# One decoder layer: a product moved forward, a residual sum cut in two, tail steps moved, a single-block unit put third

## The chip, the cores and the metric

The kernel runs on one core of a Trainium2 chip. The metric is the device time of that core in microseconds (us), from the start of the program to its end; less is better. The median of three runs before the change is 1732.85 us (1726.88, 1732.85 and 1733.94). Each kernel is also profiled once, in an execution of its own; the times of single instructions below all come from that one execution.

The engines are named as the profile names them: PE multiplies matrices (PEld is its loading of weights), DVE and ACT work elementwise, POOL does the same for a few operations, SP starts the transfers (DMA). Each engine takes its own instructions strictly in the order in which the program has them, and waits on semaphores for what the others make.

## The reference, cut to what matters

One layer of a hybrid decoder, for 1024 prompt tokens and 8 x 8 sample tokens (1088 in all), in float32:

```python
h = rmsnorm(x, g_mix_pre) * (1 + scale_m) + shift_m
proj = h @ w_in
sc_b, sc_c, sc_x, z, xbc, dt_raw = jnp.split(proj, idx, axis=-1)
y_sc = sc_b * causal_dwconv(sc_c * sc_x, sc_buf, sc_conv_w)      # short convolution
...                                                              # xbc, dt -> SSD scan -> y_ssd
y_ssd = rmsnorm(grouped(y_ssd * silu(z)), 1.0) * ssm_norm_g
mix = jnp.concatenate([y_sc, y_ssd], axis=-1) @ w_out
x = x + gate_m * rmsnorm(mix, g_mix_post)
h2 = rmsnorm(x, g_ffn_pre) * (1 + scale_f) + shift_f
f = (jax.nn.silu(h2 @ w_gate) * (h2 @ w_up)) @ w_down
x = x + gate_f * rmsnorm(f, g_ffn_post)
```

D_MODEL is 1024, the short-convolution group has 1024 channels, the SSD group 16 heads of 64 in four groups, and the hidden width of the FFN is 2816 (11 blocks of 256).

## The kernel before, in words

**Number format.** A float32 product is made of three matmuls on parts: a value v is split into `hi` (v rounded by a cast on ACT) and `lo` (v - hi, a subtraction on DVE), and hi·hi + hi·lo + lo·hi is summed in PSUM. So every weight tile costs one cast on ACT and one subtraction on DVE before PE can use it (`part`, L1039 and L1040; for whole weight columns `split_w`, L311 and L312). The third matmul of a group of three is the one that needs the `lo` part of the weight (L1080 in a product, L336 in a plain sum `acc3`).

**Units of seven products.** Most of the large matrix products are done as *units*: a 256-column strip of a weight against all tokens, cut 2 x 2, with seven half-size products instead of eight (the products are numbered 1 to 7 as in Strassen's scheme). `combos_w` (L1042) loads the strip as two `raw` tiles and makes the seven weight combinations with additions on DVE (one of them on POOL where `eng` says so) and a `part` for each; it takes the tiles from a ring (`in_turn(w_from)`). `unit` (L1082) walks the table `ORDER`, the sequence of products 1, 5, 6, 3, 7, 2, 4; for each entry and each of the two token blocks q it issues one `product` (24 or 12 matmuls, `pm` and `pz` being the PSUM tiles of block 0 and 1), and then the evacuation: a copy on ACT (L1093) or an addition on DVE (L1095). `between` names generators of other work of which one step is issued behind product n.

**Short convolution.** For each of four pairs of channel tiles three units run (`sc_unit`: the columns of sc_c at 1024, of sc_x at 2048, of sc_b at 0). Between their products stand the steps of `norm`, the grouped norm of the SSD output (groups 2 and 3 are still open when the first unit starts): squares on ACT and DVE (L929, L930), sums of squares by six-matmul groups on PE (L920), then the reciprocal root, twelve small DVE instructions (`rsqrt_of`, L279 to L285, on a tile called `sm`), and then `spread`, six-matmul groups on PE that read its result (L291). PE stands still at L291 until the last L285 is done.

**Output projection and tail.** `out_proj` runs 8 plain products for each of three token ranges (L1318 to L1321: three-part sums on PE, an addition on DVE into `acc`), and between them the steps of `mix_tail`, the tail of the mixer: transposes back to token rows (L1239), squares (L1240), a multiplication (L1241), the reciprocal root, the residual sum `x += r * u` on DVE (L1256, four tiles of 128x1024 in the first tail), the sum of squares of the new rows (L357 on ACT), their root, the scaling on ACT (L1348), transposes (L1356), and the evacuation with the FFN norm's factors on ACT (L1358). A dictionary like `{0: [tail], 2: [tail], 5: [tail]}` says behind which product the next step of a generator is issued.

**FFN.** While the tail of the last tokens runs, the first two strips of gate and up are done as plain products (`plain_step`, weights `wp`). One hidden strip of token block 1 is left over (strip 1, `(1, [1])`), then come full units (both blocks) for strips 2 to 9 and two single-block units for strip 10. Each ends in `inner_out`, which writes splits of f to DRAM (`f_d`, L1541) through SP's queue. SP also starts all loads of weight strips (`raw`, L1035) in program order, so a load stands behind every write issued before it. The full units give one of the weight sums to POOL, the single-block ones do all on DVE.

**What sets the order.** The order on PE is that of the code (`chained` and `in_order` tie each step to the PE instruction before it). On ACT and DVE the scheduler of the framework interleaves what depends on nothing earlier, by its own estimate of when an instruction is due; moving a product on PE so also moves weight preparations of ACT and DVE against other work there.

Of the kernel before, what the change touches and what calls it, by code (L numbers as in the profile page):

```python
# [16 lines left out]
P = 128  # L17
# [10 lines left out]
QS = [(0, 256), (512, 288)]  # L28
# [5 lines left out]
def hymba_step(ctx, tc, i, o):  # L34
    nc = tc.nc
# [1003 lines left out]
        nc.scalar.copy(hi, v)  # L1039
        (eng or nc.vector).tensor_tensor(lo, v, hi, op=sub)  # L1040

    def combos_w(w, cols, eng=nc.gpsimd):  # L1042
        raws = [raw_half(w, j, cols) for j in range(2)]
        a11, a12, a21, a22 = (raws[j][:, :, m * P:(m + 1) * P] for m in range(2) for j in range(2))
        W = {}

        def parts_(p, b):
            pl = in_turn(w_from)
            t = pl.tile([P, 2, 4, P], F32R, tag="wc", name=nm(f"w{p}_"))
            part(t[:, 0], t[:, 1], b)  # L1050
            W[p] = [[t[:, s, k] for k in range(4)] for s in range(2)]

        parts_(1, a11)
        parts_(4, a22)
        nc.vector.tensor_tensor(a22, a21, a22, op=add)
        parts_(5, a22)
        eng.tensor_tensor(a21, a11, a21, op=sub)
        nc.vector.tensor_tensor(a11, a22, a11, op=sub)
        parts_(6, a11)
        parts_(2, a12)  # L1060
        nc.vector.tensor_tensor(a12, a12, a11, op=sub)
        parts_(3, a12)
        parts_(7, a21)
        return W
# [14 lines left out]
            mm(ps, W[0][k], X[1][k], start=False, stop=False, skip_group_check=True)  # L1079
            mm(ps, W[1][k], X[0][k], start=False, stop=(stop and k == nk - 1), skip_group_check=True)  # L1080

    def unit(W, X, nk, qs, out, first=True, between={}, blocks_=QS, queue=in_order):  # L1082


        B = {}
        for n, (p, b, new, i, h, opens) in enumerate(ORDER):
            for q in qs:
                if new:
                    B[b, q] = (pm, pz)[q]()
                ps = B[b, q][:, :blocks_[q][1]]  # L1090
                queue(product, ps, W[p], X[q][p], nk, new, p in (3, 2, 4))
                if first and opens:
                    nc.scalar.copy(out(q, i, h), ps)  # L1093
                else:
                    nc.vector.tensor_tensor(out(q, i, h), out(q, i, h), ps, op=add)  # L1095
            for gen in between.get(n, ()):
                if queue is in_order:
                    in_order(next, gen, None)
                else:
                    next(gen, None)  # L1100
# [89 lines left out]
    sums_last()  # L1190


    def sc_unit(cols, tiles, between):
        unit(combos_w(w_in, cols, nc.vector), X_sc, 4, [0, 1],
             lambda q, i, h: tiles[i][:, SQ[q][0] + 272 * h:SQ[q][0] + 272 * (h + 1)], True, between, SQ, chained)

    kept = []
    for pr in range(4):
        cc, cx = [yt((pap, yp2)[pr % 2]) for _ in range(2)], [yt(yp4) for _ in range(2)]
        sc_unit(1024 + 256 * pr, cc, {n: [norms] for n in range(3, 7)})  # L1200
        sc_unit(2048 + 256 * pr, cx, {n: [norms] for n in range(7)})
        if pr == 2:
            conv_state(ncs, 16, 3, o["ssmc_p"], o["ssmc_s"])
        ext = []
        for m in range(2):
            ct = 2 * pr + m
            e = yt(yp4, (P, YT))
            es = e[:, 2 + NP:2 + NP + 80].rearrange("p (b t) -> p b t", b=8)
            nc.vector.tensor_tensor(e[:, 2:2 + NP], cc[m][:, :NP], cx[m][:, :NP], op=mult)
            nc.vector.tensor_tensor(es[:, :, 2:10], bt(cc[m][:, NP:]), bt(cx[m][:, NP:]), op=mult)  # L1210
            keep_tail(e, es, hscT[:, ct, :], nsc[:, ct, :], 2)
            conv(cc[m], e, es, [scw[:, j, ct:ct + 1] for j in range(3)], ct, None)
            ext.append(e)
        cb = [yt(yp4) for _ in range(2)]
        sc_unit(256 * pr, cb, {n: [norms, norms] for n in range(7)})
        for m in range(2):
            y, hi, lo = cc[m], ext[m][:, :T].bitcast(F32R), cb[m].bitcast(F32R)
            nc.vector.tensor_tensor(y, y, cb[m], op=mult)
            split(hi, lo, y)
            kept.append((2 * pr + m, hi, lo))  # L1220
        if pr < 3:
            while kept:
                y_out(*kept.pop(0))


    def size(t):
        return P if t < 8 else NS

    def residual_rows(at, ts, G, res, u, banks, done, parts=((0, 4), (4, 4)), pool=(), halves=(slice(0, D),),
                      squares=None):  # L1230
        ss = smp.tile([P, 3, 12], F32, tag="sm", name=nm("ss"))
        nc.gpsimd.memset(ss, 0.0)
        for j, (k0, nk) in enumerate(parts):
            for tt, t in enumerate(ts):
                tn = size(t)
                cols = slice(k0 * P, (k0 + nk) * P)
                ps = banks[j][tt]()[:tn, :nk * P]
                for k in range(nk):
                    nc.tensor.transpose(ps[:, k * P:(k + 1) * P], at(k0 + k, t), ident)  # L1239
                nc.scalar.activation((squares or u[tt])[:tn, cols], ps, AF.Square, accum_out=ss[:tn, j, tt:tt + 1])  # L1240
                nc.vector.tensor_tensor(u[tt][:tn, cols], ps, (G[0] if t < 8 else G[1])[:tn, cols], op=mult)  # L1241
            if j < len(parts) - 1:
                yield
        n = len(ts)
        for j in range(1, len(parts)):
            nc.vector.tensor_tensor(ss[:, 0, :n], ss[:, 0, :n], ss[:, j, :n], op=add)
        r = rsqrt_of(ss[:, 0, :n], D)
        for tt, t in enumerate(ts):
            tn = size(t)
            for cols in halves:  # L1250
                v, w = res[tt][:tn, cols], u[tt][:tn, cols]
                if tt in pool:
                    nc.scalar.activation(w, w, AF.Copy, scale=r[:tn, tt:tt + 1])
                    nc.gpsimd.tensor_tensor(v, v, w, op=add)
                else:
                    nc.vector.scalar_tensor_tensor(v, w, r[:tn, tt:tt + 1], v, op0=mult, op1=add)  # L1256
                done(t, tn, res[tt], cols)
        yield


# [74 lines left out]
    def mix_tail(ts, x_new, row_new, G):  # L1335
# [5 lines left out]
            nc.sync.dma_start(xn_d[t * P:t * P + tn, :], v[:tn, :])  # L1341
            sum_sq(v, tn, ssn, t, u[t - ts[0]])

        yield from residual_rows(lambda m, t: acc_at(m, t * P, size(t)), ts, G, xr, u, [[pz] * 4] * 2, keep)
        r = rsqrt_of(ssn[:, ts[0]:ts[-1] + 1], D)
        for tt, t in enumerate(ts):
            v = xr[tt][:size(t), :]
# [35 lines left out]
    nxt = next_splits()  # L1383
    out_proj(0, terms[0], {0: [nxt], 2: [nxt]}, out_load)
    tail = mix_tail([0, 1, 2, 3], lambda t: load_x(t, fb, "fm"), rows_fm, G_m)
    out_proj(1, terms[1], {0: [tail], 2: [tail], 5: [tail]}, out_load)
    out_proj(2, terms[2], {1: [tail], 2: [tail]}, out_load, (0, 1))


# [186 lines left out]
    out_proj(2, terms[2], {7: [tail_a]}, lambda mp: w_last, (3,))  # L1576
    tail_b = mix_tail([6, 7, 8], x_tl, row_tl, G2)
    st_from.append(pool(tailp, "stx", 1))
    plain_step(0, 0, ({0: [tail_b], 2: [tail_b], 3: [tail_a]}, {0: [tail_a], 1: [tail_a, mark()], 3: [tail_b]}))
    st_from[:] = [st0]  # L1580
    raw_from = [btp] * 4
    w_from = [slots[1]] * 4 + [slots[0]] * 4
# [23 lines left out]
            "(k p) n -> p k n", p=P))  # L1606
        return raw

    for j, qs in [(1, [1])] + [(j, [0, 1]) for j in range(2, 10)] + [(10, [0]), (10, [1])]:
        eng = nc.gpsimd if len(qs) == 2 else nc.vector  # L1610
        gate_unit(j, qs, combos_w(w_gate, 256 * j, eng))
        W = combos_w(w_up, 256 * j, eng)
# [183 lines left out]
```

## Time and profile before

| | |
|---|---|
| runs (us) | 1726.88, 1732.85, 1733.94; median 1732.85 |
| profiled execution | 1732.75 us, of which the span shown by the profile is 1731.0 us |
| mean granted clock of PE | 0.99 of full speed |
| PE busy | 1682.0 us, 97% of the span, 12604 matmuls |
| DVE, ACT, POOL busy | 1147.9 us (66%), 770.9 us (45%), 185.7 us (11%) |
| read and written | 184.63 MB and 69.71 MB, 147 GB/s over the span |

In rows of instructions the columns are: start in us from the span's start, busy us, engine, line, operation, tile written and tiles read, shapes and types, how many such instructions in a row (x4), and in brackets the idle time of the engine just before and what ended it. In rows of waits: engine, tile and line that waited, who released it, then the total us, the number of waits and the longest. In rows of windows: the stretch in us, its length, then for PE, PEld, DVE, ACT and POOL the busy us with the number of instructions, then the mean granted clock of PE, the share of DMA time, and GB/s.

### The profile page before, as it was taken

How to read it: one execution, taken by the hardware profiler on the slowest of the kernel's cores; microseconds unless marked ns; L12 is line 12 of the kernel's file. 1: busy time of each engine (PE TensorE's matmuls, PEld its weight loads, DVE VectorE, ACT ScalarE, POOL GpSimd, SP SyncE). 2: the span in 40 equal slices, each digit the busy share in tenths (PEclk: the TensorE clock that was granted, in tenths of full speed). 3: DMA queues.
4: the chain of work that ended last, by engine and by line, in shares of the span. 5: the costliest groups of instructions: out<-in, count | busy, mean ns of one | idle time of the engine just before them, and what ended most of it. 6: DMA issues, size and time to landing. Idle time of an engine off the chain costs nothing. (4 is left out here: it accounts for less than half of the span.)

```text
span 1731.0 us, 31270 instructions
## 1 busy us (share of the span) xinstructions
PE 1682.0 (97%) x12604; PEld 1600.0 (92%) x12604; DVE 1147.9 (66%) x2194; ACT 770.9 (45%) x1571; POOL 185.7 (11%) x277
## 2 busy tenths in 40 slices
PE   5999999999999999999999999999999999999997
PEld 4898888899999999998989999999999999999987
DVE  5588677777798776661037779666666658588734
ACT  3457454657544433322226676444444446422222
POOL 2110001000001000000000000122222200122112
PEclk9999999999999999999999999999999999999999
DMA  9201344442322522348275643334433438865523
GB/s 321 73 21 30 113 152 151 148 131 77 109 69 77 177 70 74 113 165 301 69 255 183 195 134 140 121 140 142 147 131 140 148 123 312 314 230 198 203 92 134
DMA packets 159624, 256.37 MB, mean 148 GB/s; under 512 B 10578, under 2 KB 123394, under 8 KB 157943
## 3 DMA queue, kind: packets, MB, share of 16 engines
q1 hardware_dynamic: 159190, 253.19, 42.9%
q8 instruction: 99, 1.62, 0.4%
q10 hardware_dynamic: 288, 1.18, 0.2%
q14 instruction: 47, 0.38, 0.1%
HBM read 184.63 MB, written 69.71 MB: 147 GB/s over the span
## 5 line engine op out<-in xcount | busy, mean ns | idle before, releaser
L312 DVE TENSOR_TENSOR wl<-raw,wh 128x512 fp32r<-128x512 f32 (+1 forms) x87 | 61.3, 729 | 100.3 <-ACT wh L311 89.2
L334 PE MATMUL pm<-h,wh 128*128 128x384 f32 (+1 forms) x342 | 115.1, 337 | 0.1
L335 PE MATMUL pm<-h,wh 128*128 128x384 f32 (+1 forms) x342 | 114.9, 336 | 0.0
L336 PE MATMUL pm<-h,wl 128*128 128x384 f32 (+1 forms) x342 | 114.3, 335 | 0.0
L336 PE MATMUL pm<-hb,wl 128*128 128x512 f32 (+2 forms) x320 | 107.3, 337 | 2.1 <-DVE wl L312 2.1
L311 ACT CAST wh<-raw 128x512 fp32r<-128x512 f32 (+1 forms) x89 | 56.4, 665 | 116.2 <-PE pm L335 68.2
L335 PE MATMUL pm<-hb,wh 128*128 128x512 f32 (+2 forms) x320 | 107.4, 337 | 0.0
L334 PE MATMUL pm<-hb,wh 128*128 128x512 f32 (+2 forms) x320 | 105.8, 338 | 1.0 <-ACT wh L311 1.0
L1039 ACT CAST wd<-raw 128x256 fp32r<-128x256 f32 x112 | 42.9, 406 | 96.1 <-PE pz L1080 33.6
L1040 DVE TENSOR_TENSOR fs<-f,fs 128x576 fp32r<-128x576 f32 (+2 forms) x76 | 52.9, 710 | 25.3 <-ACT fs L1039 24.5
L336 PEld LDWEIGHTS pm<-hb,wl 128*128 128x128 f32 x320 | 60.8, 190 | 7.6 <-DVE wl L312 2.4
L334 PEld LDWEIGHTS pm<-h,wh 128*128 128x128 f32 x342 | 65.5, 191 | 1.9 <-issue 0.9
L335 PEld LDWEIGHTS pm<-h,wh 128*128 128x128 f32 x342 | 65.3, 191 | 1.4 <-issue 0.7
L334 PEld LDWEIGHTS pm<-hb,wh 128*128 128x128 f32 x320 | 60.3, 190 | 6.8 <-ACT wh L311 1.2
L336 PEld LDWEIGHTS pm<-h,wl 128*128 128x128 f32 x342 | 65.2, 191 | 1.3 <-issue 1.0
L1078 PE MATMUL pz<-fc,wd 128*128 128x288 f32 x224 | 66.2, 295 | 0.0
L1080 PE MATMUL pz<-fc,wd 128*128 128x288 f32 x224 | 66.0, 295 | 0.0
L1079 PE MATMUL pz<-fc,wd 128*128 128x288 f32 x224 | 65.9, 294 | 0.0
L335 PEld LDWEIGHTS pm<-hb,wh 128*128 128x128 f32 x320 | 60.8, 190 | 5.2
L1078 PE MATMUL pm<-fc,wd 128*128 128x256 f32 x224 | 63.3, 283 | 1.4 <-DVE facc L1095 1.4
L1040 DVE TENSOR_TENSOR wd<-raw,wd 128x256 fp32r<-128x256 f32 x112 | 54.4, 494 | 14.6 <-ACT wd L1039 14.2
L1080 PE MATMUL pm<-fc,wd 128*128 128x256 f32 x224 | 63.1, 282 | 0.3 <-DVE wd L1040 0.3
(5568 smaller groups left out, 6203.2 us busy)
## 6 DMA issues: line engine op xcount, KB each, us to landing
raw<-in_w_in SPq DMA_DIRECT2D x48, 512.0 KB
wa<-in_w_ada SPq DMA_DIRECT2D x32, 512.0 KB
raw<-in_w_out SPq DMA_DIRECT2D x32, 512.0 KB
f_d<-fs SPq DMA_DIRECT2D x28, 576.0 KB
f_d<-fs SPq DMA_DIRECT2D x30, 512.0 KB
raw<-in_w_gate SPq DMA_DIRECT2D x28, 512.0 KB
raw<-in_w_up SPq DMA_DIRECT2D x28, 512.0 KB
y_d<-y SPq DMA_DIRECT2D x26, 544.0 KB
```

The lines of the kernel that those rows point to most:

```text
L311: (nc.gpsimd.tensor_copy if hi_eng else nc.scalar.copy)(wh, raw)
L312: (eng or nc.vector).tensor_tensor(wl, raw, wh, op=sub)
L334: mm(ps[:, :n], wh, xh, start=(first and j == 0), stop=False)
L335: mm(ps[:, :n], wh, xl, start=False, stop=False)
L336: mm(ps[:, :n], wl, xh, start=False, stop=(last and j == end))
L1039: nc.scalar.copy(hi, v)
L1040: (eng or nc.vector).tensor_tensor(lo, v, hi, op=sub)
L1078: mm(ps, W[0][k], X[0][k], start=(start and k == 0), stop=False, skip_group_check=True)
L1079: mm(ps, W[0][k], X[1][k], start=False, stop=False, skip_group_check=True)
L1080: mm(ps, W[1][k], X[0][k], start=False, stop=(stop and k == nk - 1), skip_group_check=True)
```

## The change

There are four edits.

**A.** In the first short-convolution unit (strip at column 1024 of the first pair) product 2 is done second instead of sixth: 1, 2, 5, 6, 3, 7, 4. `combos_w` makes the parts of product 2 in the second place too.

**B.** `residual_rows` may pause after the second residual sum; in the first tail of the mixer (tokens 0 to 511) it does. So that tail has one step more, and `out_proj(1, ...)` gives it steps behind products 0, 2, 4 and 5 instead of 0, 2 and 5.

**C.** In the up half of the FFN's first plain step (blocks 0 to 3), tail a had its two steps behind blocks 0 and 1, with the marker behind block 1, and tail b its step behind block 3; now tail a has them behind blocks 1 and 2, the marker stays behind block 1, and tail b's stays behind block 3.

**D.** The unit for strip 1 of token block 1 alone runs behind the full units of strips 2 and 3 instead of ahead of them.

```diff
-    def combos_w(w, cols, eng=nc.gpsimd):
+    def combos_w(w, cols, eng=nc.gpsimd, second=False):
...
         parts_(1, a11)
+        if second:
+            parts_(2, a12)
         parts_(4, a22)
...
         parts_(6, a11)
-        parts_(2, a12)
+        if not second:
+            parts_(2, a12)
         nc.vector.tensor_tensor(a12, a12, a11, op=sub)
...
-    def unit(W, X, nk, qs, out, first=True, between={}, blocks_=QS, queue=in_order):
+    def unit(W, X, nk, qs, out, first=True, between={}, blocks_=QS, queue=in_order, order=ORDER):
...
-        for n, (p, b, new, i, h, opens) in enumerate(ORDER):
+        for n, (p, b, new, i, h, opens) in enumerate(order):
...
-        sc_unit(1024 + 256 * pr, cc, {n: [norms] for n in range(3, 7)})
+
+        sc_unit(1024 + 256 * pr, cc, {n: [norms] for n in range(3, 7)},
+                ORDER if pr else ORDER[:1] + ORDER[5:6] + ORDER[1:5] + ORDER[6:])
...
                 done(t, tn, res[tt], cols)
+            if tt == pause:
+                yield
         yield
...
-        yield from residual_rows(lambda m, t: acc_at(m, t * P, size(t)), ts, G, xr, u, [[pz] * 4] * 2, keep)
+        yield from residual_rows(lambda m, t: acc_at(m, t * P, size(t)), ts, G, xr, u, [[pz] * 4] * 2, keep,
+                                 pause=1 if len(ts) == 4 else None)
...
-    out_proj(1, terms[1], {0: [tail], 2: [tail], 5: [tail]}, out_load)
+    out_proj(1, terms[1], {0: [tail], 2: [tail], 4: [tail], 5: [tail]}, out_load)
...
-    plain_step(0, 0, ({0: [tail_b], 2: [tail_b], 3: [tail_a]}, {0: [tail_a], 1: [tail_a, mark()], 3: [tail_b]}))
+    plain_step(0, 0, ({0: [tail_b], 2: [tail_b], 3: [tail_a]}, {1: [tail_a, mark()], 2: [tail_a], 3: [tail_b]}))
...
-    for j, qs in [(1, [1])] + [(j, [0, 1]) for j in range(2, 10)] + [(10, [0]), (10, [1])]:
+    for j, qs in [(j, [0, 1]) for j in (2, 3)] + [(1, [1])] + [(j, [0, 1]) for j in range(4, 10)] + [(10, [0]), (10, [1])]:
```

The lines of the changed kernel are 3 to 9 higher than before from L1055 on; below, its rows have its own lines.

**Edit A on DVE**, behind the last sums of squares of group 2: the end of the reciprocal root (tile `sm_694`, lines L283 to L285), against the parts of weights of the second and third units (`w2__701`, `w3__702`, `w7__703` and `w1__724`, `w4__725`). Before:

```order
L284 SCALAR_TENSOR_TENSOR sm_694_5499<-sm_694_5499 128x9
L285 SCALAR_TENSOR_TENSOR sm_694_5499<-sm_694_5499 128x9
L1040 TENSOR_TENSOR w2__701_5531<-raw_696_5514,w2__701_5531 128x512
L1061 TENSOR_TENSOR raw_696_5514<-raw_696_5514,raw_695_5512 128x4x128
L1040 TENSOR_TENSOR w3__702_5535<-raw_696_5514,w3__702_5535 128x512
L1040 TENSOR_TENSOR w7__703_5538<-raw_695_5512,w7__703_5538 128x512
L939 SCALAR_TENSOR_TENSOR y_291_2313<-y_291_2313,vT_1054,pz_706_5569 128x384
```

and in the changed kernel:

```order
L285 SCALAR_TENSOR_TENSOR sm_694_5499<-sm_694_5499 128x9
L1040 TENSOR_TENSOR w7__703_5538<-raw_695_5512,w7__703_5538 128x512
L283 TENSOR_TENSOR sm_694_5499<-sm_694_5499 128x9
L1040 TENSOR_TENSOR w1__724_5804<-raw_722_5800,w1__724_5804 128x512
L284 SCALAR_TENSOR_TENSOR sm_694_5499<-sm_694_5499 128x9
L1040 TENSOR_TENSOR w4__725_5807<-raw_723_5802,w4__725_5807 128x512
L285 SCALAR_TENSOR_TENSOR sm_694_5499<-sm_694_5499 128x9
L1057 TENSOR_TENSOR raw_723_5802<-raw_722_5800,raw_723_5802 128x4x128
L283 TENSOR_TENSOR sm_694_5499<-sm_694_5499 128x9
L1059 TENSOR_TENSOR raw_722_5800<-raw_722_5800 128x4x128
L284 SCALAR_TENSOR_TENSOR sm_694_5499<-sm_694_5499 128x9
L1060 TENSOR_TENSOR raw_722_5800<-raw_723_5802,raw_722_5800 128x4x128
```

The twelve small instructions stood together (with one addition of squares, L930, among them); now nine large ones stand between them, in turn, from the `lo` of w2 to the difference at L1060, and the last L285 follows behind that. On PE the first L291 stood between products 1 and 5 of the second unit, and now stands between the two token blocks of its product 5.

**Edit B on DVE**, in the output projection of tokens 512 to 815: the four residual sums, two additions of product tiles into `acc1`, and the `lo` parts of the next weights. Before:

```order
L1256 SCALAR_TENSOR_TENSOR x_1037_9330<-y_1041_9338,sm_1062_9469,x_1037_9330 128x1024
L1256 SCALAR_TENSOR_TENSOR x_1038_9332<-y_1042_9339,sm_1062_9469,x_1038_9332 128x1024
L1256 SCALAR_TENSOR_TENSOR x_1039_9334<-y_1043_9340,sm_1062_9469,x_1039_9334 128x1024
L1256 SCALAR_TENSOR_TENSOR x_1040_9336<-y_1044_9341,sm_1062_9469,x_1040_9336 128x1024
L1321 TENSOR_TENSOR acc1_8208<-acc1_8208,pm_1070_9536 128x304
L1321 TENSOR_TENSOR acc1_8208<-acc1_8208,pm_1071_9562 128x304
L312 TENSOR_TENSOR wl_1076_9610<-raw_1073_9605,wh_1075_9609 128x512
```

and in the changed kernel:

```order
L1262 SCALAR_TENSOR_TENSOR x_1037_9330<-y_1041_9338,sm_1062_9469,x_1037_9330 128x1024
L1262 SCALAR_TENSOR_TENSOR x_1038_9332<-y_1042_9339,sm_1062_9469,x_1038_9332 128x1024
L1329 TENSOR_TENSOR acc1_8208<-acc1_8208,pm_1070_9530 128x304
L1262 SCALAR_TENSOR_TENSOR x_1039_9334<-y_1043_9340,sm_1062_9469,x_1039_9334 128x1024
L1262 SCALAR_TENSOR_TENSOR x_1040_9336<-y_1044_9341,sm_1062_9469,x_1040_9336 128x1024
L1329 TENSOR_TENSOR acc1_8208<-acc1_8208,pm_1071_9562 128x304
L312 TENSOR_TENSOR wl_1076_9610<-raw_1073_9605,wh_1075_9609 128x512
```

One addition has moved in between the second and the third residual sum; the same six stand ahead of the `lo` part.

**Edit C on ACT**, from the evacuations of the first transposes of tail a (tokens 512 to 767) to the cast of the next plain weights (`wp__1191`; `fs` are the output splits of f, `x` the rows of tail b that are scaled). Before:

```order
L1358 ACTIVATE acc1_8208<-pz_1179_10409,modT_280,A_f_4798 128x256
L1348 ACTIVATE x_1146_10144<-x_1146_10144,sm_1182_10465 128x1024
L1348 ACTIVATE x_1147_10146<-x_1147_10146,sm_1182_10465 128x1024
L1348 ACTIVATE x_1148_10148<-x_1148_10148,sm_1182_10465 64x1024
L1039 CAST fs_1184_10485<-f_1138_10101 128x256
L1039 CAST wp__1191_10507<-raw_1189_10503 128x512
```

and in the changed kernel:

```order
L1039 CAST fs_1184_10485<-f_1138_10101 128x256
L1367 ACTIVATE acc1_8208<-pz_1177_10423,modT_280,A_f_4798 128x256
L1367 ACTIVATE acc1_8208<-pz_1178_10427,modT_280,A_f_4798 128x256
L1367 ACTIVATE acc1_8208<-pz_1179_10431,modT_280,A_f_4798 128x256
L1367 ACTIVATE acc1_8208<-pz_1180_10435,modT_280,A_f_4798 128x256
L1357 ACTIVATE x_1146_10144<-x_1146_10144,sm_1182_10465 128x1024
L1357 ACTIVATE x_1147_10146<-x_1147_10146,sm_1182_10465 128x1024
L1357 ACTIVATE x_1148_10148<-x_1148_10148,sm_1182_10465 64x1024
L1039 CAST fs_1183_10481<-f_1138_10101 128x512
L1039 CAST wp__1191_10507<-raw_1189_10503 128x512
```

A cast of f (128x256) moves from behind the three scalings to between the two groups of four evacuations, and a larger one (128x512) takes its place ahead of the weight's cast. On PE the first group of transposes of tail a stood behind block 0 of the up half, the second behind block 1; now the first stands behind block 1 and the second behind block 2.

More of the change, by code (lines that the diff above doesn't have):

```diff
@@ L1190, in hymba_step, with sc_unit @@
     sums_last()
-    def sc_unit(cols, tiles, between):
-        unit(combos_w(w_in, cols, nc.vector), X_sc, 4, [0, 1],
-             lambda q, i, h: tiles[i][:, SQ[q][0] + 272 * h:SQ[q][0] + 272 * (h + 1)], True, between, SQ, chained)
+    def sc_unit(cols, tiles, between, order=ORDER):
+        unit(combos_w(w_in, cols, nc.vector, order is not ORDER), X_sc, 4, [0, 1],
+             lambda q, i, h: tiles[i][:, SQ[q][0] + 272 * h:SQ[q][0] + 272 * (h + 1)], True, between, SQ, chained,
+             order)
     kept = []
@@ L1229, in residual_rows @@
     def residual_rows(at, ts, G, res, u, banks, done, parts=((0, 4), (4, 4)), pool=(), halves=(slice(0, D),),
-                      squares=None):
+                      squares=None, pause=None):
         ss = smp.tile([P, 3, 12], F32, tag="sm", name=nm("ss"))
```

## The prediction

> **What bounds the kernel now.** I read the page's busy times first, then PE's waits, then the windows around each wait.
>
> ```profile
> PE 1682.0 (97%) x12604; PEld 1600.0 (92%) x12604; DVE 1147.9 (66%) x2194; ACT 770.9 (45%) x1571; POOL 185.7 (11%) x277
> ```
>
> PE is busy 97% of the span: 49 us of idle in all. The change takes away no matmul and adds none, so it can only win idle time of PE, or time in which PE runs at a lower clock. The waits of PE that lie at the four places (total us, count, longest):
>
> ```profile
> PE pm L336 <- DVE wl L312: 2.5, 2, 2.1
> PE pz L1356 <- ACT x L1348: 2.5, 2, 2.1
> PE pm L1080 <- DVE w__680_5275 L1040: 1.0, 1, 1.0
> PE pm L1078 <- ACT w__680_5275 L1039: 1.0, 1, 1.0
> PE pz L1078 <- DVE f L1095: 0.9, 1, 0.9
> PE pz L1080 <- DVE w__1267_11172 L1040: 0.7, 1, 0.7
> ```
>
> The first belongs to edit B, the second to C, the next two to A (w__680 is product 6 of the first unit), the last two to D. Together 8.6 us. Behind the longer ones more is lost; in these windows column two is PE's busy time, and the number ahead of the last two the granted clock:
>
> ```profile
> 508.99:512.40 3.41, 1.98 (x13) 1.76 (x14) 3.41 (x7) 3.08 (x6) 0.00 (x0) 0.98 0.02 5
> 512.40:515.81 3.41, 3.41 (x17) 3.41 (x17) 3.41 (x6) 0.77 (x2) 0.00 (x0) 0.52 0.75 224
> 993.56:996.97 3.41, 1.51 (x12) 1.28 (x12) 3.41 (x6) 3.10 (x4) 0.00 (x0) 1.00 0.31 127
> 996.97:1000.38 3.41, 3.41 (x19) 3.41 (x18) 1.15 (x4) 3.41 (x9) 0.00 (x0) 0.50 0.80 257
> ```
>
> In a stretch of 3.41 us PE was busy for 1.98 or 1.51; in the next 3.41 us the clock was about half. PE did about 1.7 us of work in it, so such a dip costs 1.7 us more than the stall.
>
> The Trainium skill, "TensorE: Matmul & The Clock Gate", section "HAM oscillation — how this bites in real kernels", gives the rule "no PE-idle gaps >~3.4µs". The trace agrees on the length of a window and not on the trigger: idle of 1.4 to 1.9 us in one window was enough. What the rule would make of the sum is among the rivals.
>
> **Edit A, the first unit.** Rows of PE and DVE there:
>
> ```profile
> 502.18 0.29 PE L1078 MATMUL pm<-bt,w__677_5263 128*128 128x272 f32 x1
> 505.18 0.29 PE L1078 MATMUL pm<-x__636_4870,w__679_5270 128*128 128x272 f32 x1
> 510.20 0.69 DVE L1040 TENSOR_TENSOR w__680_5275<-raw,w__680_5275 128x512 fp32r<-128x512 f32 x1
> 529.94 0.29 PE L1078 MATMUL pm<-bt,w__697_5516 128*128 128x272 f32 x1
> 532.94 0.83 PE L291 MATMUL pz<-ident,sm 128*128 128x128 f32 x6
> 533.53 0.37 PE L1078 MATMUL pm<-x__636_4870,w__699_5523 128*128 128x272 f32 x1
> ```
>
> One product takes 505.18 - 502.18 = 3.0, a six-matmul group 533.53 - 532.94 = 0.6. The unit has seven products and three groups at L920: 7 x 3.0 + 3 x 0.6 = 22.8. It took 529.94 - 502.18 = 27.8. Nearly 5 are lost: 2.0 of waits, 1.7 of dip, the rest small; I take 4.8. After the change the `lo` of product 6 comes one part later, 510.20 + 0.6, and ends at about 511.5; PE, with product 2 ahead, wants it at 502.18 + 9.0 + 0.25 = 511.4. So this stall goes, and its dip. The second unit then starts at about 524.3 (before 529.94; one of the three groups has moved behind its start).
>
> But the work that the stall gave time to is then late. What is late next is L291, which reads the reciprocal root:
>
> ```profile
> 527.54 0.17 DVE L279 TENSOR_SCALAR sm<-pz 128x9 f32<-128x9 f32 x1 [0.57 <-PE pz L920]
> 530.27 0.17 DVE L285 SCALAR_TENSOR_TENSOR sm<-sm 128x9 f32<-128x9 f32 x1
> ...
> 568.48 0.69 DVE L1040 TENSOR_TENSOR w__753_6096<-raw,w__753_6096 128x512 fp32r<-128x512 f32 x1
> 569.09 0.16 DVE L283 TENSOR_TENSOR sm<-sm 128x9 f32<-128x9 f32 x1
> 569.16 0.68 DVE L1040 TENSOR_TENSOR w__754_6099<-raw,w__754_6099 128x512 fp32r<-128x512 f32 x1
> ...
> 570.19 0.16 DVE L285 SCALAR_TENSOR_TENSOR sm<-sm 128x9 f32<-128x9 f32 x1
> 570.41 2.27 PE L291 MATMUL pz<-ident,sm 128*128 128x128 f32 x18
> ```
>
> Before, the chain took 530.44 - 527.54 = 2.9 and was ready 2.5 ahead of L291 at 532.94. Now nine large instructions stand in it. The later norm shows the price of a large and a small one in turn, 569.16 - 568.48 = 0.68, and that PE follows the last L285 within 0.1 (570.35 to 570.41). So: L279 at 524.3 + 0.5 + 0.6 + 0.2 = 525.6; nine pairs 6.1, the addition of squares 0.5, three small ones left 0.6: ready at 532.8. PE arrives at 524.3 + 3.0 + 1.5 + 0.6 = 529.4: it stands for about 3.4. It resumes at 532.8, and 0.6 later has done what stood done at 533.53 + 1.5 = 535.0 before: 1.6 gained. An idle of 3.4 takes at least half of a window whichever way it falls, more than the 1.4 that was enough, so a dip follows: 1.7 lost. **A: about 0.** Bounds: -4.8 if the root is in time, +1.0 if the chain is 1 us longer.
>
> **Edit B.**
>
> ```profile
> 931.50 4.88 DVE L1256 SCALAR_TENSOR_TENSOR x<-y,sm,x 128x1024 f32<-128x1024 f32 x4
> 936.29 0.84 DVE L1321 TENSOR_TENSOR acc<-acc,pm 128x304 f32<-128x304 f32 x2
> 937.06 1.28 DVE L312 TENSOR_TENSOR wl<-raw,wh 128x512 fp32r<-128x512 f32 x2
> 937.79 0.41 PE L336 MATMUL pm<-hb,wl 128*128 128x304 f32 x1 [2.13 <-DVE wl L312]
> ```
>
> DVE runs without a gap from 931.50 to the `lo` for which PE waits. The change puts one of the two L1321 between the sums; the same 4.88 + 0.84 stands ahead of L312. **B: 0**: the stall of 2.1 stays, and a dip behind it if one is there as behind the other two. Bounds: 0 and -3.8 (2.1 + 1.7), for no row gets longer.
>
> **Edit C.**
>
> ```profile
> 993.87 2.19 ACT L1348 ACTIVATE x<-x,sm 128x1024 f32<-128x1024 f32 x2 [3.04 <-DVE sm L285]
> 995.07 0.66 PE L1356 MATMUL pz<-ident,x 128*128 128x128 f32 x4 [2.11 <-ACT x L1348]
> ...
> 999.08 1.90 ACT L1358 ACTIVATE acc<-pz,modT,A_f 128x256 f32<-128x256 f32 x4
> 1001.38 1.93 ACT L1358 ACTIVATE acc<-pz,modT,A_f 128x256 f32<-128x256 f32 x4 [0.40 <-PE pz L1356]
> 1003.51 3.23 ACT L1348 ACTIVATE x<-x,sm 128x1024 f32<-128x1024 f32 x3 [0.20 <-issue]
> 1006.65 0.39 ACT L1039 CAST fs<-f 128x256 fp32r<-128x256 f32 x1
> 1006.95 0.62 ACT L1039 CAST wp__1191_10507<-raw 128x512 fp32r<-128x512 f32 x1
> ...
> 1008.62 0.38 PE L336 MATMUL pm<-x__1114_9935,wp__1191_10507 128*128 128x256 f32 x1 [0.50 <-DVE wp__1191_10507 L1040]
> ```
>
> PE now does block 1 of the up half ahead of the first transposes, so of the 2.1 + 0.4 for x about 0.4 is left. But from 993.87 to 1007.5 ACT works all but through (0.4 and 0.2 idle): scaling, squares, evacuations, scaling, then the cast of `wp__1191`, and PE cannot go on without that. The change loses ACT the 0.4 of idle and swaps a 0.3 cast for a 0.5 one: the cast ends 0.1 to 0.3 earlier. So what PE loses here, waits of 2.5 + 0.5 and the dip's 1.7, becomes 0.4 for x, some 0.7 for PSUM tiles that ACT empties late, and a wait of about 3.4 in front of `wp__1191`, with the end 0.3 earlier. And the dip, which until now fell at 997, where PE had to wait for ACT afterwards anyway, then falls behind the last wait: 1.7 lost that was free. **C: +1.4** (-0.3 + 1.7). Bounds: -4.2 (both waits and a dip) if ACT's row is not what holds, +2.4 if the dip is long.
>
> **Edit D.**
>
> ```profile
> 1059.78:1084.47 24.69, 23.07 (x170) 22.44 (x169) 22.64 (x42) 15.05 (x29) 1.61 (x1) 1.00 0.49 170
> 1084.47:1126.77 42.30, 42.30 (x338) 42.30 (x337) 28.02 (x47) 18.42 (x37) 4.86 (x3) 1.00 0.34 112
> ```
>
> First row: the single-block unit of strip 1; second: the full units of strip 2. The single one halves PE's work and keeps DVE's weight work: DVE is busy 22.64 of 24.69 and PE loses 1.6 idle and some 0.7 of restarts. The full one has PE without a gap and DVE at two thirds. Put third, the single unit finds its weights prepared in the slack of strips 2 and 3, since the ring holds parts of more than one unit. A full strip at once after the plain steps asks half as much of DVE per us. **D: -2.1.** Bounds: -2.3 (all that was lost) and +2.3 (the same loss again at its new place and as much at strip 2's start). SP has the loads and writes in a new order:
>
> ```profile
> 1135.18 10.43 SPq L1541 DMA_DIRECT2D f_d<-fs  x6
> 1151.87 1.02 SPq L1035 DMA_DIRECT2D raw<-in_w_up  x2
> ```
>
> Strip 3 starts at 1126.77, and the loads of the up half next but one go out at 1151.87, 25.1 later, behind the writes of strip 2. Put behind the single unit, these are wanted after 24.7 - 2.3 + 21.2 = 43.6 (half of 42.30 for one full gate half): 18.5 between. The loads take about 5 by the transfer times there, a cast and a subtraction 1.3, so some 12 are to spare.
>
> **Sum.** 0 + 0 + 1.4 - 2.1 = -0.7. The profiled execution took 1732.75, 0.1 below the median of the runs: **1732.0**.
>
> **The rivals.**
>
> *One chain is in time.* If DVE's chain in A runs ahead of its order's price (small instructions in the shadow of large ones), A is worth -4.8: 1732.75 - 4.8 + 1.4 - 2.1 = 1727.2. If instead ACT is 4 us earlier at `wp__1191`, C is -4.2 and the time 1726.4. For it: PE's arrival at L291 is worked out to 0.5 only. Against: DVE and ACT have no idle rows in those chains.
>
> *The stalls come, the dips don't.* Against it stand the two windows shown, for it that a stall which falls across two windows may leave each with less idle than 1.4 if it is shorter than worked out. Then A is -1.6 and C -0.3: 1732.75 - 1.6 - 0.3 - 2.1 = 1728.7. By the rule of the Trainium skill named above the time would come out so, as both new stalls are no longer than its 3.4.
>
> *All four do what they say.* A -4.8, C -4.2, D -2.3: 1721.4; with B's -3.8, 1717.6. For it: all these waits are in the rows. Against: it needs both engines' chains to shrink, and no instruction is removed.
>
> *Slower: the single unit starves between full ones.* Place: the gate and up loads of strip 4 on SP's queue, behind strip 3's writes, wanted half as long after as before. It decides from about 12 us of lateness; with 20, PE stands 8 more and has a dip, D is +9.7 in place of -2.1: 1743.8. For it: the writes at 1135.18 hold SP's queue for 10.43. Against: the slack above.
>
> **Chances.** Forecast 0.57; one chain in time 0.16; no dips 0.10; all four 0.12; slower 0.05. The single times of before lie 7 us apart, so about 0.5% (8.7 us) is what a measurement can tell from no change: faster is below 1724.2, slower above 1741.5. Faster is the fourth rival and little else, 0.13; slower the last, 0.04; same 0.83. The forecast's own range is 1728 to 1736 (A and C at their upper bounds, D at zero; the lower end by the spread of the runs). The range for 8 in 10 takes in the second and third cases and half of the fourth: 1723 to 1738.
>
> **What would show it.** A right: no wait at product 6 of the first unit, the second unit at about 524, a wait of 3 to 4 at L291 there, and a clock near 0.5 behind it; wrong if L291 starts without one. B right: a wait of 2.1 for `wl` stays at about the same place. C right: a wait near 3.4 for `wp__1191` in place of that for x, and a dip behind it. D right: no waits at weights in the first units, nor in the single one; wrong if its windows again hold less than full PE. The whole is wrong if the waits at these places shrink together, or a new one for `raw` shows up behind strip 3.

## The result, and the profile after

The changed kernel takes 1741.95 us (median of 5 runs, 1737.74 to 1743.37), before it 1732.85. The ratio is 1.0054, with a 95% interval of 1.0038 to 1.0071, so 6.6 to 12.3 us slower. The forecast was 1732.0, with 1723 to 1738 as its range: the time lies outside.

The page of the changed kernel, its busy times:

```profile
PE 1683.9 (97%) x12604; PEld 1602.1 (92%) x12604; DVE 1146.7 (66%) x2194; ACT 770.3 (44%) x1571; POOL 195.1 (11%) x277
```

PE does the same matmuls. Its idle time grew by 3.6, from 49.0 (1731.0 - 1682.0) to 52.6 (1736.5 - 1683.9), and its busy time by 1.9, from 1682.0 to 1683.9. PE's waits at the four places:

```profile
PE pz L1081 <- ACT f L1096: 6.3, 1, 6.3
PE pz L291 <- DVE sm L285: 3.2, 1, 3.2
PE pm L334 <- ACT wp__1191_10507 L1039: 3.0, 1, 3.0
PE pm L336 <- DVE wl L312: 2.5, 2, 2.1
```

The second, third and fourth are those that the prediction named: 3.2 at L291 (forecast 3.4), 3.0 at wp__1191 (3.4), 2.1 for wl (2.1). The first was not forecast. It stands in the single-block unit of strip 1. PE's rows, each the first matmul behind its wait, in the order A, B, C, D:

```profile
531.52 0.80 PE L291 MATMUL pz<-ident,sm 128*128 128x128 f32 x2 [3.18 <-DVE sm L285]
...
936.46 0.41 PE L336 MATMUL pm<-hb,wl 128*128 128x304 f32 x1 [2.13 <-DVE wl L312]
...
1004.83 0.39 PE L334 MATMUL pm<-x__1114_9935,wp__1191_10507 128*128 128x256 f32 x1 [2.95 <-ACT wp__1191_10507 L1039]
...
1163.65 0.61 PE L1081 MATMUL pz<-x__1243_10982,w__1362_12254 128*128 128x288 f32 x1 [6.32 <-ACT f L1096]
```

Windows of the changed kernel (PE's busy time is the second number, the granted clock stands ahead of the last two): the full strips 2 and 3, the single unit of strip 1 behind them, three stretches behind its wait, and the stretch behind the wait at wp__1191.

```profile
1058.22:1142.83 84.61, 84.61 (x675) 84.61 (x673) 56.19 (x96) 39.65 (x80) 11.83 (x11) 1.00 0.38 128
1142.83:1174.21 31.38, 25.06 (x170) 24.82 (x169) 23.27 (x35) 16.24 (x31) 11.35 (x10) 0.89 0.55 192
1163.65:1167.00 3.35, 3.35 (x14) 3.35 (x15) 1.88 (x4) 1.94 (x5) 1.27 (x1) 0.50 0.69 274
1169.00:1169.50 0.50, 0.50 (x5) 0.50 (x4) 0.10 (x1) 0.00 (x0) 0.00 (x0) 0.72 0.00 0
1169.50:1170.00 0.50, 0.50 (x6) 0.50 (x6) 0.35 (x1) 0.35 (x1) 0.00 (x0) 1.00 0.00 0
...
1005.29:1008.70 3.41, 3.11 (x15) 3.07 (x15) 3.41 (x8) 2.28 (x5) 0.00 (x0) 0.52 0.41 159
```

Strips 2 and 3 run without a gap, as the full units did before. The single unit, 24.7 us before, now takes 31.4, and has a dip behind its wait. The clock is back at full speed only between 1169.0 and 1169.5, so PE runs at half clock for some 5.6 us behind the wait and loses 2.8 by it, more than the 1.7 that the prediction gave to a dip.

**Where the time went.** Five marks on PE cut the execution at the places: the start of the first short-convolution unit, of product 6 of the second unit, the end of the wait for wl, the end of the plain steps, and the start of strip 4's gate unit. Between them lie the edits A, B, C and D.

```
               A       B       C       D    median    ratio to before, 95%
before       35.0   400.6   122.0   109.2
changed      35.2   400.8   121.8   116.0   1741.95   1.0054 [1.0038, 1.0071]
```

A, B and C together moved by 0.2 us, D by 6.8.

**What the single unit waits for.** The engine rows of the changed kernel, ACT first, then the end of the output on POOL and DVE. Strip 3's last product ends at 1142.83 or shortly behind it.

```profile
1143.32 0.93 ACT L1039 CAST fs<-f 128x512 fp32r<-128x512 f32 x2
...
1148.20 0.63 ACT L1039 CAST fs<-f 128x512 fp32r<-128x512 f32 x1
...
1150.17 0.62 ACT L1039 CAST fs<-f 128x512 fp32r<-128x512 f32 x1 [1.35 <-POOL f L1560]
1152.28 0.67 ACT L1039 CAST fs<-f 128x576 fp32r<-128x576 f32 x1 [1.49 <-DMA f_d<-fs]
...
1158.86 0.67 ACT L1039 CAST fs<-f 128x576 fp32r<-128x576 f32 x1 [0.37 <-POOL f L1557]
...
1161.25 0.67 ACT L1039 CAST fs<-f 128x576 fp32r<-128x576 f32 x1 [1.21 <-POOL f L1560]
1163.20 0.70 ACT L1096 COPY f<-pz 128x288 f32<-128x288 f32 x2 [1.27 <-DVE fs L1040]
```

```profile
1156.27 1.18 POOL L1556 TENSOR_TENSOR f<-f 128x288 f32<-128x288 f32 x1 [6.13 <-DVE fs L1040]
...
1160.10 1.12 POOL L1560 TENSOR_TENSOR f<-f 128x288 f32<-128x288 f32 x1
```

```profile
1162.36 0.75 DVE L1040 TENSOR_TENSOR fs<-f,fs 128x576 fp32r<-128x576 f32 x1
```

The splits with 512 columns belong to token block 0, those with 576 and 288 to block 1. Strip 3's output is a chain from engine to engine: cast, subtraction, four differences on POOL, casts and subtractions of these, each into a staging tile that an earlier write must have left. Block 1 comes second and is through at 1163.11, 20.3 us behind strip 3's last product. Only then can the copy at 1163.20 put the first product of the single unit's up half into an f tile of block 1, for there is one such tile (`f_from[1]`, one buffer). The gate half covers 11.2 us of the 20.3, two products 3.2; then both PSUM tiles are taken and PE stands.

The same could be read from the trace of before: strip 2's last product ended at 1126.77 there, and the last part of its block 1, on DVE, began at

```profile
1144.52 0.75 DVE L1040 TENSOR_TENSOR fs<-f,fs 128x576 fp32r<-128x576 f32 x1
```

so it was done 18.5 us behind. The next strip's gate half took 21.2 us and hid it. A single-block gate half is half as long.

### The profile page after: what moved, and what is told of

It is laid out like the page before. It is cut to its first block, busy times and chain, and to the rows that moved or that the text cites. A ratio compares the mean times of both kernels' runs of the same rounds, so it can differ in the third digit from the quotient of the medians.

```text
span 1736.5 us, 31272 instructions
## 1 busy us (share of the span) xinstructions
PE 1683.9 (97%) x12604; PEld 1602.1 (92%) x12604; DVE 1146.7 (66%) x2194; ACT 770.3 (44%) x1571; POOL 195.1 (11%) x277
```

## The experiments

Ten kernels, beside the kernel before on the same chip; the kernels of one group share its runs (medians 1730.88, 1730.85 and 1730.72). Each is compared with the kernel before of its own group. The expectations reckon from 1732.85, 2 us higher, so it is their differences that count.

### D alone

```diff
-    for j, qs in [(1, [1])] + [(j, [0, 1]) for j in range(2, 10)] + ...
+    for j, qs in [(j, [0, 1]) for j in (2, 3)] + [(1, [1])] + [(j, [0, 1]) for j in range(4, 10)] + ...
```

> Edit D alone, all else as before. In the two traces the stretch from the end of the plain steps to the start of strip 4 took 109.2 us before and 116.0 us after, with a wait of 6.3 us at the third product of the single unit's up half. Theory: D by itself brings this: the f tile of token block 1 has one buffer, and strip 3's output, which reads it, is done late; so 116 us here too, the wait again 6 to 6.5 us, and the time 1732.85 + 6.8 = about 1739.6. Rival (the loss comes from the four edits together): the stretch takes 107 to 109 and the time is 1731 to 1733.

1736.49 us, ratio 1.0041 [1.0027, 1.0055], so 4.7 to 9.5 us slower (6.8 expected). D took 115.3 us; PE's wait:

```profile
PE pz L1078 <- ACT f L1093: 6.3, 1, 6.3
```

It is the same wait to a tenth. The loss belongs to D and needs none of the other edits.

### A, B and C without D

The changed kernel with the loop of units as before.

> Edits A, B and C without D. By the two traces the stretch of A went from 35.0 to 35.2 us (first unit's start to product 6 of the second), that of B and what lies before it by +0.1, that of C by -0.2. Theory: these three come to nothing, each stall being moved and not removed; time within 1 us of 1732.85. Rival: the medians lie 9.1 apart and the trace shows only 6.8 at D, so A to C cost the other 2.3 in most executions: 1735.

1731.42 us, ratio 0.9999 [0.9985, 1.0013]. A 36.3, B 400.9, C 120.2, D 108.7. The three edits come to nothing, within 2.6 us. The rival's loss of 2.3 us lies just at the upper end of the interval, and the places show no such loss: A, B and C together took 657.4 us here and 657.6 before.

### Block 1 first in strip 3's output

```diff
-        for q in qs:
+        for q in (qs[::-1] if j == 3 else qs):
             v = F[q].rearrange("p m h c -> p (m h c)")
```

> The changed kernel, and in the output of strip 3 token block 1 goes first and block 0 second (they were in the other order). Nothing is left out. Theory (the single unit's evacuation waits for the f tile of block 1, which strip 3's output holds for 20.4 us after its last product because block 0 is served first): block 1's share is done some 10 us earlier, the wait of 6.3 us and the dip behind it go, the stretch takes 107 to 108 in place of 116, the time is 1741.95 - 8.5 = about 1733.5. Rival (the writes of f to DRAM on SP's queue, or their staging tiles, are the limit): the same writes leave in the same time, and a wait of 3 us or more stays.

1734.39 us, ratio 1.0025 [1.0012, 1.0038], so 3.5 above its own before by the medians, where the expectation was 0.7 above. D took 110.3 (107 to 108 expected): the wait of 6.3 is gone, and three small ones are left.

```profile
1153.19 0.40 PE L1081 MATMUL pz<-x__1243_10982,w__1349_12129 128*128 128x288 f32 x1 [0.33 <-ACT sg L1096]
1165.67 0.40 PE L1081 MATMUL pz<-x__1243_10982,w__1362_12254 128*128 128x288 f32 x1 [1.05 <-ACT f L1096]
1173.56 0.40 PE L1081 MATMUL pz<-x__1259_11133,w__1360_12245 128*128 128x288 f32 x1 [1.26 <-DVE f L1098]
```

At the place of the 6.32 stands 1.05. The writes are the same, only the order of the two blocks is not: what held the tile was block 0's turn ahead of block 1's. The work of block 0's output, now second, stands between the single unit's own copies and additions on ACT and DVE, and costs a part of what was won. Another 1.1 lies in A, which took 36.3 in place of 35.2: the dip behind L291 lasts twice as long in this trace.

### Two f tiles for block 1

```diff
-    sg_from[1], f_from[1] = ([pool(right, n, 1, side="right")] for n in ("sg1", "f1"))
+    sg_from[1], f_from[1] = ([pool(right, n, b, side="right")] for n, b in (("sg1", 1), ("f1", 2)))
```

> The changed kernel with two buffers in place of one for the f tile of token block 1. Theory: as with the order swapped, the wait of 6.3 us goes and the stretch takes 107 to 108 us, time about 1733.5. Rival (staging tiles or the write queue): the single unit's own output then still waits behind strip 3's, and strip 4's start moves by less than 4 us.

1733.0 us, ratio 1.0008 [0.9990, 1.0026]. D took 109.0 (107 to 108 expected), 7.0 less than in the changed kernel. The copies of products 1 and 5 no longer wait. The third does, by ACT's order; its row on ACT and the one ahead of it, and what PE shows:

```profile
1164.06 0.67 ACT L1039 CAST fs<-f 128x576 fp32r<-128x576 f32 x1 [1.74 <-POOL f L1560]
1164.64 0.39 ACT L1096 COPY f<-pz 128x288 f32<-128x288 f32 x1
```

```profile
1165.09 0.40 PE L1081 MATMUL pz<-x__1258_11130,w__1365_12264 128*128 128x288 f32 x1 [1.83 <-ACT f L1096]
```

The tile was the cause of the 6.3; behind it lies a second, smaller one: a cast of strip 3's output waits for POOL, and the copy that PE needs is queued behind that cast.

### Two f tiles, and strip 3's differences on DVE

```diff
-            inner_out(j, q, F[q], eng)
+            inner_out(j, q, F[q], nc.vector if j == 3 else eng)
```

> The changed kernel with two buffers for the f tile of block 1, and the four differences of strip 3's output on DVE in place of POOL. With two buffers alone a wait of 1.8 us was left, at the copy of product 6 on ACT, which stands in ACT's order behind a cast of strip 3's output that waits for POOL. Theory: with DVE in POOL's place the casts come earlier and the wait goes; from the end of the plain steps to strip 4 107.1 us (109.2 before, 116.0 with the change, 109.0 with two buffers alone). Rival (the staging tiles and the writes to DRAM hold the casts): the wait stays at 1.5 to 2 us.

1731.41 us, ratio 0.9998 [0.9986, 1.0011]. D took 106.9, 2.3 less than before the change, and holds no gap:

```profile
1061.55:1168.43 106.88, 106.88 (x843) 106.88 (x842) 73.01 (x127) 51.04 (x103) 13.12 (x12) 1.00 0.42 148
```

By this, D is worth -2.3 against the trace of before and -1.9 against the four other traces without edit D (108.7 to 108.8): the -2.1 that the prediction gave it, but only once the output of strip 3 is out of the way.

### A, with the norm's steps one product later

```diff
-        sc_unit(2048 + 256 * pr, cx, {n: [norms] for n in range(7)})
+        sc_unit(2048 + 256 * pr, cx, {n: [norms] for n in (range(7) if pr else range(1, 7))})
```

(with A alone of the four edits.)

> Edit A alone, with the steps of the norm one product later in the second unit (so that L291 stands behind product 5 and not behind product 1). Theory (A takes away 4.8 us and gives them back because PE reaches L291 3.2 us before the reciprocal root is there, with a dip behind it): with 3 us more of work ahead of L291 the wait falls to 0.3 or less and no dip follows; from the first unit's start to product 6 of the second 29.5 to 30.5 us (35.0 before, 35.2 with the change; one six-matmul group of 0.6 now lies behind product 6), time 4 to 5 below before. Rival (DVE is the limit there, so that the weights of the second unit are late next): waits at L1083 or L1081 of the second unit of 2 us or more, stretch above 32.

1728.46 us, ratio 0.9987 [0.9975, 0.9998], so 0.3 to 4.3 faster. A took 29.2 (35.0 before); two six-matmul groups, 1.2, now lie behind its end, so 4.6 are won there, and L291 waits for nothing. But B took 405.7 in place of 400.6: beyond the 1.2 that moved, 3.9 came back. Where, in PE's row:

```profile
561.46 0.59 PE L1081 MATMUL pm<-h,w__728_5816 128*128 128x272 f32 x1 [1.43 <-ACT w__728_5816 L1039]
```

and the windows of this kernel ahead of it and behind it:

```profile
546.90:557.99 11.09, 11.09 (x91) 11.09 (x91) 11.09 (x18) 4.31 (x11) 3.12 (x8) 1.00 0.26 103
...
561.46:564.90 3.44, 3.44 (x15) 3.44 (x16) 2.74 (x7) 0.21 (x1) 0.00 (x0) 0.50 0.69 203
...
567.00:567.50 0.50, 0.50 (x4) 0.50 (x4) 0.50 (x3) 0.00 (x0) 0.00 (x0) 0.50 0.00 0
568.00:568.50 0.50, 0.50 (x6) 0.50 (x5) 0.14 (x1) 0.00 (x0) 0.00 (x0) 1.00 0.00 0
```

From 546.9 to 558.0 DVE works without a gap on the short convolution's own elementwise work; the weights of the third unit come behind it, and PE, now earlier, meets them 1.4 too early, with a dip behind that lasts past 567.5: some 6.4 us at half clock, 3.2 lost. The theory of L291 holds; the expected 4 to 5 did not come, because the next chain on DVE was as late. Over A and B 0.7 is left in this trace (434.9 against 435.6).

### B, with the later two sums behind product 6

```diff
-    out_proj(1, terms[1], {0: [tail], 2: [tail], 4: [tail], 5: [tail]}, out_load)
+    out_proj(1, terms[1], {0: [tail], 2: [tail], 6: [tail], 7: [tail]}, out_load)
```

(on A, B and C without D.)

> Edits A, B, C without D, and in B the third and fourth residual sums are given to the step behind product 6 (scaling behind 7) in place of 4 and 5. On DVE two sums and one addition then stand ahead of the lo part that PE waits for, in place of four and two. Theory (the wait of 2.1 us is DVE's row of four sums): wait for wl 0.9 or less, no dip behind it; from product 6 of the second unit to the end of the plain steps 3 to 4 us less than the 400.8 + 121.8 of the changed kernel, if the tail's later steps still have slack. Rival (PE waits for the cast on ACT or for the wh buffer): the wait keeps 1.5 us or more.

1732.79 us, ratio 1.0007 [0.9993, 1.0021]. The wait of 2.1 for wl is gone. B and C together took 521.6 us (521.1 with A, B and C alone, 522.5 in the changed kernel): nothing is won. The waits have moved to the scaled rows of the same tail:

```profile
948.77 0.66 PE L1365 MATMUL pz<-ident,x 128*128 128x128 f32 x4 [1.00 <-ACT x L1357]
949.81 0.65 PE L1365 MATMUL pz<-ident,x 128*128 128x128 f32 x4 [0.39 <-ACT x L1357]
950.85 0.65 PE L1365 MATMUL pz<-ident,x 128*128 128x128 f32 x4 [0.39 <-ACT x L1357]
951.89 0.66 PE L1365 MATMUL pz<-ident,x 128*128 128x128 f32 x4 [0.39 <-ACT x L1357]
```

The wait was DVE's row of sums, as the theory says; the slack of the later steps, which it counted on, is not there.

### C, with tail b's scaling in the next step

```diff
-    plain_step(0, 0, (..., {1: [tail_a, mark()], 2: [tail_a], 3: [tail_b]}))
+    plain_step(0, 0, (..., {1: [tail_a, mark()], 2: [tail_a]}))
...
-    plain_step(1, 0, ({0: [tail_b], 1: [tail_b]}, ...))
+    plain_step(1, 0, ({0: [tail_b], 1: [tail_b], 2: [tail_b]}, ...))
```

(on A, B and C without D.)

> Edits A, B, C without D, and in C the scaling of tail b (three instructions on ACT, 3.2 us) moves from behind block 3 of the up half into the next plain step. Theory (the wait of 3 us at wp__1191 is ACT's row of work ahead of its cast): the wait falls to 0.3 or less, no dip there, and the stretch from the wait for wl to the end of the plain steps takes about 117.5 us in place of 121.8 (before 122.0). Rival (the raw weights or DVE are late there): the wait stays above 1.5 or comes back as a wait of the same length for x in the next step.

1728.39 us, ratio 0.9988 [0.9977, 0.9999]. C took 117.7 (117.5 expected; 120.2 with A, B and C alone, 122.0 before). The wait at wp__1191 is gone, and of the waits for x 0.16 is left:

```profile
999.46 0.98 PE L1365 MATMUL pz<-ident,x 128*128 128x128 f32 x7 [0.16 <-ACT x L1357]
```

ACT's row was the limit at C.

### The mended edits together

A, C and D as mended above (two f tiles and DVE for strip 3), B as before the change.

> The three mended edits together, B left as before: A with the norm's steps one product later, C with tail b's scaling in the next step, D with two buffers for f of block 1 and strip 3's differences on DVE. By the places of the single runs: A (first unit to the wait for wl) -0.7 to -1.9, C -4.2, D -2.3; if they add, 7.5 to 8.5 below before, about 1722.5 to 1723.5. Rival (what is won at one place is lost at the next, as in A): 3 to 4 below before and a new wait of 2 us or more between the places.

1723.59 us, ratio 0.9960 [0.9947, 0.9974], so 4.5 to 9.2 us faster (7.5 to 8.5 expected). A 29.2, B 403.3, C 117.5, D 106.9: from the first unit to strip 4 656.9 us, 10.0 less than before. The places add; the new wait of 1.4 for the third unit's weights stays, but no dip follows it here, and so B took 2.4 less than with A alone. The profiled execution is one of the fastest of the six (1720.35 us), and its stretches show more than the medians, which lie 7.1 apart.

### The same with B

```diff
-    out_proj(1, terms[1], {0: [tail], 2: [tail], 5: [tail]}, out_load)
+    out_proj(1, terms[1], {0: [tail], 2: [tail], 6: [tail, tail]}, out_load)
...
-    out_proj(2, terms[2], {1: [tail], 2: [tail]}, out_load, (0, 1))
+    out_proj(2, terms[2], {2: [tail], 3: [tail]}, out_load, (0, 1))
```

(and the pause after the second sum.)

> As the kernel before this one, and B too: the third and fourth residual sums and the scaling behind product 6, the two steps of transposes behind products 2 and 3 of the next part in place of 1 and 2. Theory: the wait of 2.1 us for wl and its dip go, and with one product more ahead of the transposes the waits of 2.2 us for x that the later sums brought go too: 2 to 3.5 us below the kernel without it, about 1720. Rival (the tail's chain is as long as its slack): waits for x or at the first plain products of 2 us or more, no gain.

1718.85 us, ratio 0.9938 [0.9922, 0.9954], so 8.0 to 13.5 us faster than before, and faster than the changed kernel too. From the first unit to strip 4 it took 656.5 us, 0.3 less than without B. The waits for wl and for the scaled rows are gone, and another stands between, for the rows of tail b:

```profile
982.97 1.22 PE L1245 MATMUL pz<-ident,acc 128*128 128x128 f32 x8 [1.76 <-DVE tl L1247]
```

The medians of the two kernels lie 4.7 apart, the places only 0.3. The two traces also differ in where dips fall: without B there is one behind the wait for wl, with B one behind the wait for the third unit's weights. That B itself gains is not shown.

## Why the prediction was wrong, point by point

All stretches in one table (us; B + C where a kernel has no wait for wl to cut at):

```
                               A      B      C       D
before                       35.0  400.6  122.0   109.2
changed                      35.2  400.8  121.8   116.0
D alone                      35.0  400.6  120.0   115.3
A, B, C                      36.3  400.9  120.2   108.7
changed, block 1 first       36.3  401.4  121.9   110.3
changed, two f tiles         35.4  400.6  122.5   109.0
changed, two f tiles, DVE    35.3  400.6  122.2   106.9
A alone, norm later          29.2  405.7  120.8   108.8
A, B, C, B later             35.3     521.6       108.8
A, B, C, C later             35.4  400.8  117.7   108.8
mended A, C, D               29.2  403.3  117.5   106.9
mended A, B, C, D            29.2     520.5       106.9
```

**D is the step that failed.** The prediction gave -2.1, with -2.3 and +2.3 as bounds. Measured: +6.8 in the changed kernel, +6.0 alone. The 6.8 is the sum of 6.3 of waiting, 2.8 of dip and the -2.3 of the weights; alone, the dip leaves PE 4.0 us at half clock, and 6.3 + 2.0 - 2.3 is the 6.0. It asked of the moved unit whether its weights and its loads would be ready, and they were: no wait for a weight or a load is left in it. It did not ask what the unit writes into. Its f tile is held by the output of the strip ahead, which ends 18.5 us behind that strip in the trace of before and 20.3 in the changed one; the prediction moved the unit from behind a plain step to behind a full strip, and thereby from a free tile to a held one. The upper bound was taken from the loss at the old place, not from this row. What it said of the weights was right, since with the tile and strip 3's output out of the way D is worth -2.3.

**The rival on the slower side** had the place, the single unit between the full ones, but another mechanism (late loads of strip 4) and 0.05 of the chance. No wait for a load shows there; loads for strip 4's up half went out at 1158.20. That its time, 1743.8, comes near the 1741.95 is luck: by its own terms D would have been 8 + 1.7 - 2.1 = +7.6 and not +9.7, and none of the 8 was there.

**A** (about 0, bounds -4.8 and +1.0): +0.2 in the changed kernel; over the seven traces with A and the norm's steps at their old place 35.2 to 36.3, over the two without A 35.0. Right, and by the steps given: no wait at product 6 of the first unit, second unit 22.4 us behind the first (forecast 524.3 - 502.18 = 22.1), the wait at L291 3.2 (3.4), a dip behind. The two traces at 36.3 are those in which this dip lasts twice as long. That the wait is the interleaved root is shown by the later norm, which removes it.

**B** (0): right, the wait is 2.13 and 2.13, and a dip follows it in both traces (clock 0.50 from about 938.9 to 942.3 before, from 937.2 to 940.6 in the changed kernel); the sums are its cause, since it goes when two of them stand behind wl.

**C** (+1.4): the wait at wp__1191 was 3.0 in place of 3.4 and had its dip. ACT's rows in the changed kernel, and PE's last row for this weight:

```profile
991.39 2.19 ACT L1357 ACTIVATE x<-x,sm 128x1024 f32<-128x1024 f32 x2 [2.90 <-DVE sm L285]
...
1004.13 0.64 ACT L1039 CAST wp__1191_10507<-raw 128x512 fp32r<-128x512 f32 x1
...
1005.63 0.58 PE L336 MATMUL pm<-x__1114_9935,wp__1191_10507 128*128 128x256 f32 x1 [0.30 <-DVE wp__1191_10507 L1040]
```

From the scaling to the cast ACT took 12.7 in place of 13.1 (1006.95 - 993.87), so the cast is 0.3 earlier, as forecast; from PE's row to the end of the plain steps it took 52.6 in place of 51.2 (1008.62 to 1059.78), 1.4 more, where 1.7 was forecast for the dip. That the earlier dip was free holds only in part: in the trace of D alone, which has none there, ACT's stretch took 12.2. In this pair of traces C as a whole is -0.2, because the stretch ahead of ACT's scaling was 1.2 shorter; no step of edit C stands in it, and in the trace of D alone it was as short; over the kernels without a mended C, the three without edit C took 120.0 to 122.0, the five with it 120.2 to 122.5. Means 120.9 and 121.7: nearer to the forecast, and smaller than the spread. Right in its steps; the size over the whole stretch is not settled.

**The sum** was -0.7; with D at +6.8 in place of -2.1 and the others as forecast it would have been 1732.75 + 8.2 = 1741.0, against 1741.95 measured; so close an agreement is partly luck, as C was not +1.4 in this pair. The changed kernel's stretches explain 6.9 of the 9.1 between the medians; the rest is within the interval.

**The rival "all four do what they say"** was a matter of one step more at each place. The mended kernel with B lies 11.9 below its own before by the medians, and 8.0 to 13.5 by the interval; the rival named 11.4 to 15.2 below. Without B, A and B together keep 3.1 (432.5 against 435.6) of A's 4.8.

**The other two rivals** did not come: neither chain was in time, and the clock fell to half behind both new stalls (0.50 from 531.0 to 534.4, and the row at 1005.29 above).

## What to carry to other kernels

When a piece of work is moved, go through what it writes as well as what it reads: who holds that buffer at the new place, and when the trace shows it released. A cover such as a 21 us gate half that hides an 18.5 us output has no row of its own in a profile; it shows only when something shorter is put in its place. And a stall that is taken away shows the next chain, which was as late and hidden: move that as well, or nothing is won.

## What the runs showed of the hardware that was not expected

Whether a dip of the granted clock follows a wait, and how long it lasts, is not settled by the length of the wait. The wait of 2.1 us for wl stands in ten of the twelve traces. In seven of them the clock falls to 0.50 behind it for about 3.4 us; in three (A, B and C without D; block 1 first; A with the later norm) it stays at 1.00. The changed kernel, and A, B and C without D, each from 0.75 us behind the end of this wait:

```profile
937.21:940.61 3.40, 3.40 (x16) 3.40 (x15) 2.56 (x8) 2.09 (x5) 0.00 (x0) 0.50 0.75 253
936.25:939.65 3.40, 3.40 (x27) 3.40 (x26) 3.35 (x11) 3.03 (x7) 0.00 (x0) 1.00 0.73 246
```

Behind the wait of 1.43 us for the third unit's weights the clock was at half for 6.8 us with A alone, for 3.4 in the mended kernel with B, and not at all in the one without B. Behind 1.83 us in the kernel with two f tiles it stayed at 1.00:

```profile
1165.10:1168.50 3.40, 3.40 (x26) 3.40 (x27) 2.45 (x5) 1.60 (x3) 1.20 (x1) 1.00 1.01 388
```

What decides was not found. So two traces of the same code can differ at one place: B took 405.7 with A alone and 403.3 in the mended kernel without B, whose code is the same up to there.

The Trainium skill, "TensorE: Matmul & The Clock Gate", section "HAM oscillation — how this bites in real kernels", names gaps over about 3.4 us as what is to be avoided; in these runs less than half of that could suffice, and did not always.

The first short-convolution unit, ahead of which no kernel here is changed, started between 498.25 and 505.25 us in the twelve profiles: 7 us, where single runs of the kernel before lie 10 us apart in one group (1726.73 to 1736.92). This is why stretches between marks were compared here and not single times.
